# Seven y products behind the gates of a recurrent layer, and a front with its sines on GpSimd

## The chip, the cores and the metric

The kernel runs on one core of a Trainium2 chip, as one launch. The metric is the device time of that core in microseconds (us). The engines are named PE (TensorE), DVE (VectorE), ACT (ScalarE), POOL (GpSimd) and SP (SyncE, which here only starts transfers).

## What is computed

Two blocks act on 256 tokens of width 1024. The first has an attention layer with low-rank queries and keys (MLA), a state-space layer (SSM) and an MLP after each; each of the four parts has a shift, a scale and a gate that come from the vector c (modulation). The second has a recurrent layer, an attention layer and four feed-forward layers (f10, f20, f11, f21). Everything is fp32.

```python
def mla_mixer(h, cos, sin, w_in, q_norm, w_qb, kv_norm, w_kvb, w_o):
    z = h @ w_in                                  # 256 x (256 + 128 + 64)
    cq, ckv = rms_norm(z[..., :256], q_norm), rms_norm(z[..., 256:384], kv_norm)
    k_pe = apply_rope(z[..., 384:], cos, sin)
    # q from cq @ w_qb, keys and values from ckv @ w_kvb, 8 heads, causal softmax
    return o @ w_o

def rg_lru(x, w_r, b_r, w_i, b_i, lam):           # four heads of 256 x 256
    r, i = sigmoid(x @ w_r + b_r), sigmoid(x @ w_i + b_i)
    log_a = -LRU_C * r * softplus(-lam)
    u = sqrt(-expm1(2.0 * log_a)) * (i * x)
    return scan(exp(log_a), u)                    # along the tokens

def recurrent_block(xn, ...):
    xb, yb = split(xn @ w_in + b_in)
    h = rg_lru(causal_dwconv(xb, conv_w, conv_b), w_r, b_r, w_i, b_i, lam)
    return (h * gelu(yb)) @ w_out + b_out
```

## The kernel before, in words

All weights arrive as units of 128 x 1024 (512 KB), in one order that `plan()` writes down (L97). SP starts their transfers from one place, `_issue` (L404 to L418), into seven buffers `raw` taken in turn; a buffer is free again once its unit has been processed. `run` (L426) processes the next units: a unit "w" is split into a high half (`wh`, ACT, L458) and a low half (`wl`, DVE, L464; a few on POOL, L462), in a ring of eleven slots; a unit "m" of a modulation matrix is multiplied by silu(c) and summed on DVE (L522), which gives one column of shift, scale or gate; a unit "p" is a weight of the MLA front with a buffer of its own; a unit "x" stays in its raw buffer (`take_kept`). A product with split weights takes three matmuls: `wh` with the high half of the activations (`hh` or `xh`), `wl` with it, and `wh` with their low half (`hl` or `xl`). `step` and `take` (L474, L488) call `run` until a unit is there. What an engine does in which order follows from the program's order.

The front. `setup` (L946) makes silu(c), the decay of the SSM (`ssm_decay`, two powers on POOL), the angles and their sines and cosines (`sincos`, L909, on DVE, with Sin on ACT), the rope tables by 16 copies on POOL (L1001 to L1005), and the powers of the SSM's transition by 71 small operations on POOL (`ssm_powers`, L1281). `mla` (L1061) then takes eight pairs of modulation units; each pair gives one of eight groups of x, scaled, for PE's product with w_in. Norms of the result use `rpow` (L651), a power on POOL. Behind it stand on POOL the rotations of the SSM (`ssm_inputs`, L1351): tables of cosines and sines for two halves of the tokens, doubled in six steps of six operations each, 72 in all. SP stores them with `store` (L1355), at points that `tick` sets while the heads run. `ssm_tables` (L1333) turns the result of the powers by two transposes on PE (the wt transposes), and SP stores them.

The heads (`heads`, L1198) follow a string of tokens, `HEADS0`, repeated for each head with lags: T turn, S scores, B maximum (DVE), A product with the values, E exponential (ACT), N norm (L1231, DVE), q the next pair of queries with its rope, t a tick, and a number for so many calls of units. After them come the last product of the layer, mla_o (half 0 and half 1 of the tokens, eight weight units), a layer norm per half, and mlp0. Seven modulation units of `MODS0` (`MODS_PRE`) stand in the plan between mla_o and mlp0; the other 17 are woven into mlp0.

The recurrent layer (`lru`, L1744) follows `LRU_SEQ`. X evacuates the products of lru_x, C is the convolution (DVE, L1790), Y a pair of y products (PE, 32 matmuls with kept weights), R and I the gates (PE, then ACT), A weighs x by i (L1832), Q square roots (ACT), M scales (L1840, L1843), S is the scan (L1848), E evacuates y, G is its gelu (L1709 to L1711 on DVE, with ACT between), T multiplies the scan with gelu(y) and writes `hh` (L1853, L1854), L writes `hl` (L1859), J loads a row, and a number processes so many units, here of lru_out. The product with lru_out follows, half 0 and then half 1, each with an epilogue that begins at L708.

Of the kernel before, what the change touches and what calls it, by code (L numbers as in the profile page):

```python
# [36 lines left out]
LRU_SEQ = "X0 X1 C0 X2 C1 X3 Y0 E0 R0 I0 C2 R1 I1 C3 A0 R2 I2 A1 R3 I3 A2 Y1 Y2 Y3 H0 G0 A3 Q0 Q1 Q2 Q3 1 M0 S0 E1 M1 S1 G1 1 M2 S2 T0 T1 1 L0 E2 M3 S3 G2 1 L1 T2 J1 1 E3 G3 L2 1 J0 T3 J2 1 L3 1"  # L37
HEADS0 = "T2 S0 B0 1 A2 E0 N0 t q t 1"
# [46 lines left out]
LRU_W = _w("lru_x", 8) + [("x", "lru_y", 0), ("x", "lru_y", 1)] + [("x", "lru_" + c, k) for k in range(2) for c in "ri"]  # L85
LRU_W += [("x", "lru_y", k) for k in range(2, 8)] + _w("lru_out", 8)
MODS0 = _mod(2, 0) + _mod(2, 1) + _mod(1, 2)
MODS_AT = 8
MODS_PRE = 7
# [7 lines left out]
def plan():  # L97
# [218 lines left out]
class Model:  # L316
    def __init__(self, ctx, tc, ws, cols, rows, x, pos, inv, rel, sp, sbc, sgb, out):
# [30 lines left out]
        self.mhalf = T("mhalf", [128, 4])  # L348
        self.lri = T("lri", [128, 8], I32)
# [13 lines left out]
        self.pend = deque()  # L363
        self.kept = {}
# [3 lines left out]
        self.fill = 0  # L368

# [34 lines left out]
    def _issue(self, limit):  # L404
        while self.ndma < min(limit, len(UNITS)):
            j = self.ndma
            u = UNITS[j]
            if u[0] == "p":
                dst = self.pt[u]
            else:  # L410
                r = RPOS[j]
                if r >= RAWN and RUNITS[r - RAWN] >= self.nproc:
                    return
                dst = self.raw[r % RAWN]
                if any(dst is x for x, _ in self.pend) or any(dst is x for x in self.kept.values()):
                    return
# [9 lines left out]
    def run(self, look=LOOK, maxn=99, mods=2):  # L426
        n = 0
        while self.nproc < len(UNITS) and n < maxn:
# [4 lines left out]
            if u[0] == "m":  # L433
                if mods == 0 or (self.hold and self.modfin is not None):
                    break
                mods -= 1
# [4 lines left out]
            self.settle(KEEP)  # L441
            if u[0] == "w":
# [7 lines left out]
                if own is None and s >= RING - 3 and self.early:  # L450
                    break
# [11 lines left out]
                else:  # L463
                    self.nc.vector.tensor_tensor(self.Ls[s], raw, self.f32(self.Hs[s]), op=OP.subtract)  # L464
# [41 lines left out]

    def settle(self, keep):
# [401 lines left out]
    def sincos(self, s, c, ang, t1, t2):  # L909
        nc = self.nc  # L910
        tau = 2.0 * math.pi
# [3 lines left out]
        nc.vector.tensor_scalar(t1, ang, 1.0 / tau, MAGIC, op0=OP.mult, op1=OP.add)  # L915
        nc.vector.tensor_scalar(t1, t1, -MAGIC, None, op0=OP.add)
        nc.vector.scalar_tensor_tensor(t2, t1, -c1, ang, op0=OP.mult, op1=OP.add)
        nc.vector.scalar_tensor_tensor(t2, t1, -c2, t2, op0=OP.mult, op1=OP.add)
        nc.vector.scalar_tensor_tensor(t2, t1, -c3, t2, op0=OP.mult, op1=OP.add)
        nc.vector.tensor_scalar(t2, t2, 3.1415925, -3.1415925, op0=OP.min, op1=OP.max)  # L920
        nc.scalar.activation(s, t2, func=AF.Sin)
        nc.scalar.activation(t1, t2, func=AF.Sin, scale=0.5)
        nc.vector.scalar_tensor_tensor(t1, t1, -2.0, t1, op0=OP.mult, op1=OP.mult)
        nc.vector.tensor_scalar(c, t1, 1.0, None, op0=OP.add)
# [21 lines left out]
    def setup(self):  # L946
# [3 lines left out]
        spt = self.Z[1][:, 1664:1664 + NSP]  # L950
        inv = self.Z[1][:, 1600:1632]
# [12 lines left out]
        V.memset(self.mhalf, -0.5)  # L964
        jp = self.Z[0][:, 0:128]
# [14 lines left out]
        while self.nproc < 2:  # L980
            self.step()
        V.tensor_copy(self.identb, self.ident)
        V.tensor_copy(self.maskb, self.mask)
        posf = self.stat(2)
        V.tensor_copy(posf, posi)
        n = 64 + 7 * 32
        a, t1, t2 = (self.Z[1][:, n * i:n * i + n] for i in range(3))
        sc = self.Z[1][:, 3 * n:5 * n].rearrange("p (e a) -> p e a", e=2)
        for h in range(2):
            V.tensor_scalar(a[:, 32 * h:32 * h + 32], inv, posf[:, h:h + 1], None, op0=OP.mult)  # L990
        for e in range(7):
            V.tensor_scalar(a[:, 64 + 32 * e:96 + 32 * e], self.sw[2], float(1 << (e + 1)) if e else 1.0, None, op0=OP.mult)
        self.sincos(sc[:, 0], sc[:, 1], a, t1, t2)
        self.tok = self.sb.tile([128, 2, 2, 32], F32, name="tok")
        for e in range(2):
            G.tensor_copy(self.tok[:, e], sc[:, 1 - e, 0:64].rearrange("p (h f) -> p h f", h=2))
        CT, ST = self.B2, self.BR
        for h in range(2):
            for j in range(4):
                o = slice(128 * h + 32 * j, 128 * h + 32 * j + 32)  # L1000
                G.tensor_copy(CT[:, o], self.tok[:, 0, h])  # L1001
                if j % 2 == 0:
# [1046 lines left out]
```

## Time and profile before

| | us |
|---|---|
| median of three runs | 1716.37 |
| lowest and highest | 1714.93, 1719.49 |
| the profiled execution | 1720.69 |
| its span | 1718.9 |
| PE busy | 1602.1 (93%) |
| DVE busy | 1134.9 (66%) |
| ACT busy | 832.9 (48%) |
| POOL busy | 227.1 (13%) |

A busy share is a mean over stages. PE is busy nearly all the time, so a loss is a stretch in which PE is not, and a wait on another engine counts where PE waits behind it in the end. POOL's work lies almost wholly in the first 110 us. In the rows below, a bracket at the end of a row gives the idle time of that engine just before, and what ended it; xN joins equal instructions in a row.

### The profile page before, as it was taken

What the parts mean: (1) busy time and instruction counts of PE and PEld (TensorE: products, weight loads), DVE (VectorE), ACT (ScalarE), POOL (GpSimd) and SP (SyncE); (2) the same over time, 40 slices, a digit from 0 to 9 for tenths busy, and PEclk for the clock granted to TensorE, in tenths of its full rate; (3) what the DMA queues carried; (4) which work ended last, traced back from release to release, by engine and by line L of the source; (5) the groups of instructions that cost most, each with busy time, mean ns of one, the idle gap of its engine ahead of it and who ended that gap; (6) DMA issues with size and microseconds to landing.
All of it is one profiled execution on the core that took longest, in us unless ns stands there. A gap on an engine that the chain in (4) does not pass through costs nothing.

```text
span 1718.9 us, 24910 instructions
## 1 busy us (share of the span) xinstructions
PE 1602.1 (93%) x9594; PEld 1414.2 (82%) x9594; DVE 1134.9 (66%) x1596; ACT 832.9 (48%) x1256; POOL 227.1 (13%) x318
## 2 busy tenths in 40 slices
PE   4779999998789999999999889999999999899998
PEld 2557889887778899789997758999899998779997
DVE  6688898669978655776555577555755555775553
ACT  2333657745345655353444755444544444654341
POOL 8940000003514000100000011000000001320000
PEclk9869999998899999999999999999999999999999
DMA  9477688957566665475551446565555653545540
GB/s 363 173 271 261 222 290 297 316 191 281 208 220 231 234 216 192 146 248 206 191 175 51 161 170 241 193 208 181 187 180 194 222 199 109 184 143 205 205 147 26
DMA packets 106586, 349.62 MB, mean 203 GB/s; under 512 B 12385, under 2 KB 22753, under 8 KB 106466
## 3 DMA queue, kind: packets, MB, share of 16 engines
q1 hardware_dynamic: 106466, 348.02, 58.1%
q8 instruction: 75, 1.23, 0.3%
q14 instruction: 45, 0.37, 0.1%
HBM read 338.41 MB, written 9.57 MB: 202 GB/s over the span
## 4 chain that ended last, share of the span: by engine, by line
PE 49%; DVE 4%; ACT 3%; issue 2%; POOL 1%; DMA 0%; DVEq 0%; POOLq 0%; ACTq 0%
PE bank L395 48%; DVE wl L464 1%; ACT wh L458 1%; PE bank L611 1%; ACT junka L660 1%; DMA raw<-in_ws_dram 0%; DVE r L698 0%; ACT r L1815 0%; POOL wl L462 0%; ACT z L1816 0%; PE bank L877 0%; POOL st L656 0%; DVE z L1231 0%; DVE z L1848 0%; DVE st L1218 0%
## 5 line engine op out<-in xcount | busy, mean ns | idle before, releaser
L464 DVE TENSOR_TENSOR wl<-raw,wh 128x1024 fp32r<-128x1024 f32 x456 | 549.8, 1240 | 167.9 <-ACT wh L458 166.6
L458 ACT ACTIVATE wh<-raw 128x1024 fp32r<-128x1024 f32 x472 | 478.7, 1051 | 249.5 <-PE bank L395 129.9
L395 PE MATMUL bank<-xh,wh 128*128 128x256 f32 x1664 | 472.0, 284 | 0.0
L395 PE MATMUL bank<-xh,wl 128*128 128x256 f32 x1664 | 471.2, 283 | 0.0
L395 PE MATMUL bank<-xl,wh 128*128 128x256 f32 x1664 | 470.3, 283 | 0.0
L395 PEld LDWEIGHTS bank<-xl,wh 128*128 128x128 f32 x1664 | 318.9, 192 | 2.1
L395 PEld LDWEIGHTS bank<-xh,wh 128*128 128x128 f32 x1664 | 317.9, 191 | 2.4 <-issue 0.2
L395 PEld LDWEIGHTS bank<-xh,wl 128*128 128x128 f32 x1664 | 317.5, 191 | 0.0
L395 PE MATMUL bank<-wh,hh 128*128 128x512 f32 x736 | 295.5, 402 | 6.9 <-ACT hh L1854 3.6
L395 PE MATMUL bank<-wl,hh 128*128 128x512 f32 x736 | 292.9, 398 | 1.6 <-DVE wl L464 1.5
L395 PE MATMUL bank<-wh,hl 128*128 128x512 f32 x736 | 243.9, 397 | 7.2 <-DVE hl L1859 4.4
L395 PEld LDWEIGHTS bank<-wh,hl 128*128 128x128 f32 x736 | 140.0, 191 | 40.7 <-DVE hl L1859 6.3
L395 PEld LDWEIGHTS bank<-wh,hh 128*128 128x128 f32 x736 | 141.4, 192 | 38.2 <-ACT hh L603 4.3
L395 PEld LDWEIGHTS bank<-wl,hh 128*128 128x128 f32 x736 | 141.2, 192 | 31.3 <-DVE wl L464 2.9
L522 DVE SCALAR_TENSOR_TENSOR junk<-raw,cs 128x1024 bf16<-128x1024 f32 x96 | 124.4, 1296 | 10.8 <-DMA raw<-in_ws_dram 9.6
L395 PE MATMUL bank<-wl,xh 128*128 128x512 f32 x320 | 127.0, 397 | 2.2 <-DVE wl L464 1.3
L656 POOL TENSOR_TENSOR st<-st,mhalf 128x1 f32<-128x1 f32 (+1 forms) x33 | 22.8, 692 | 798.4 <-DVE st L664 696.5
L395 PE MATMUL bank<-wh,xh 128*128 128x512 f32 x320 | 127.6, 399 | 0.7 <-ACT wh L458 0.7
L604 DVE TENSOR_TENSOR hl<-z,hh 128x512 fp32r<-128x512 f32 x68 | 47.0, 692 | 100.5 <-ACT hh L603 100.5
L395 PE MATMUL bank<-wh,xl 128*128 128x512 f32 x320 | 102.3, 397 | 5.6 <-DVE xl L604 5.6
L603 ACT ACTIVATE hh<-z 128x512 fp32r<-128x512 f32 x68 | 43.0, 632 | 106.1 <-DVE z L896 105.1
L462 POOL TENSOR_TENSOR wl<-raw,wh 128x256 fp32r<-128x256 f32 x64 | 60.6, 979 | 128.5 <-ACT wh L458 128.3
(381 smaller groups left out, 1665.3 us busy)
## 6 DMA issues: line engine op xcount, KB each, us to landing
raw<-in_ws_dram SPq DMA_DIRECT2D x580, 512.0 KB
early<-in_ws_dram SPq DMA_DIRECT2D x10, 512.0 KB
grow<-in_rows_dram SPq DMA_DIRECT2D x9, 512.0 KB
brow<-in_rows_dram SPq DMA_DIRECT2D x6, 512.0 KB
ophh<-ops_d SPq DMA_DIRECT2D x6, 512.0 KB
ophl<-ops_d SPq DMA_DIRECT2D x6, 512.0 KB
gate<-in_rows_dram SPq DMA_DIRECT2D x5, 512.0 KB
tab_d<-early SPq DMA_DIRECT2D x4, 512.0 KB
```

Source lines behind the costliest of these rows:

```text
L395: self.nc.tensor.matmul(out, l, r, start=start, stop=stop)
L458: self.nc.scalar.activation(self.Hs[s], raw, func=AF.Copy)
L462: self.nc.gpsimd.tensor_tensor(self.Ls[s][:, w], raw[:, w], self.f32(self.Hs[s])[:, w], op=OP.subtract)
L464: self.nc.vector.tensor_tensor(self.Ls[s], raw, self.f32(self.Hs[s]), op=OP.subtract)
L522: nc.vector.scalar_tensor_tensor(self.junk, raw, 1.0, self.cs, op0=OP.mult, op1=OP.mult, accum_out=total)
L603: self.nc.scalar.activation(hdst, src, func=AF.Copy)
L604: self.nc.vector.tensor_tensor(ldst, src, self.f32(hdst), op=OP.subtract)
L611: self.nc.tensor.transpose(b[:, 128 * j:128 * j + 128], src[:, 128 * k:128 * k + 128], self.ident)
L656: self.nc.gpsimd.tensor_tensor(r, v, self.mhalf[:, 0:n], op=OP.pow)
L660: self.nc.scalar.activation(self.junka[:, 0:512], src, func=AF.Square, scale=scale, accum_out=s[:, n:n + 1])
```

## The change

It has five parts.

1. The recurrent layer. The eight units of lru_out become kept units ("x"), between those of y. One y product instead of two stands ahead of the gates, seven behind them; Y is now a single product. A new letter K splits a kept unit of lru_out: K0 to K3, among the gates, with both halves on DVE, K4 to K7 with the high half on ACT. E and G come later, and L (the low half of the product's left operand, the remainder) comes late.
2. The front. The angles are made on ACT, the sines and cosines on POOL (Sin stays on ACT), the rope tables by six copies on ACT. On POOL the first three steps of rotations of one half precede `rpow`; the other rotations, a power and the 71 operations follow it. SP stores the rotations after the heads. The wt transposes move from ahead of the heads to the norm of mla_o's half 0.
3. The plan. Modulation units, front weights and units of mla_o alternate; `MODS_PRE` is 0, so that all 24 units of `MODS0` are woven into mlp0.
4. The heads process three units per head, no ticks, and delay each low half of a weight to the next unit (`lag`); their norm goes to ACT.
5. The transposes ahead of kvk are issued together, six first, and the two for the roped key after kvk.

```diff
-LRU_SEQ = "X0 X1 C0 X2 C1 X3 Y0 E0 R0 I0 C2 R1 I1 C3 A0 R2 I2 A1 R3 I3 A2 Y1 Y2 Y3 H0 G0 A3 Q0 Q1 Q2 Q3 1 M0 S0 E1 M1 S1 G1 1 M2 S2 T0 T1 1 L0 E2 M3 S3 G2 1 L1 T2 J1 1 E3 G3 L2 1 J0 T3 J2 1 L3 1"
-HEADS0 = "T2 S0 B0 1 A2 E0 N0 t q t 1"
+LRU_SEQ = "X0 X1 C0 Y0 X2 C1 X3 R0 I0 C2 R1 I1 C3 A0 K0 K1 R2 I2 A1 R3 I3 K2 K3 A2 A3 Y1 Y2 Y3 Y4 Y5 Y6 Y7 H0 0 Q0 Q1 Q2 Q3 M0 S0 M1 S1 E0 G0 K4 M2 S2 T0 E1 G1 K5 M3 S3 T1 J1 K6 E2 G2 T2 J2 L0 L1 K7 L2 E3 G3 J0 T3 L3 1 1"
+HEADS0 = "T2 S0 B0 1 A2 E0 1 N0 q 1"
...
-MODS_PRE = 7
+MODS_PRE = 0
...
-    o += [("p", "kvk", 0), ("p", "kvv", 0)]
...
+    m, w = _mod(1, 0) + _mod(1, 1) + _mod(0, 2), _w("mla_o", 8)
+    o += m[:3] + [("p", "kvk", 0), ("p", "kvv", 0)] + m[3:8] + [("p", "qb", 0)] + m[8:10]
+    o += [("p", "qb", k) for k in (1, 2, 3)] + m[10:11]
+    m = m[11:]
+    for k in range(8):
+        o += [w[k]] + m[2 * k:2 * k + 2]
...
+    def split_kept(self, tag, k, eng):
...
+        if eng is None:
+            self.nc.scalar.activation(self.Hs[s], raw, func=AF.Copy)
+        else:
+            eng.tensor_copy(self.Hs[s], raw)
+        self.nc.vector.tensor_tensor(self.Ls[s], raw, self.f32(self.Hs[s]), op=OP.subtract)
...
-        nc.vector.tensor_scalar(t1, ang, 1.0 / tau, MAGIC, op0=OP.mult, op1=OP.add)
...
+        G.tensor_scalar(t1, ang, 1.0 / tau, MAGIC, op0=OP.mult, op1=OP.add)
+        G.tensor_scalar(t1, t1, -MAGIC, None, op0=OP.add)
+        for x in (c1, c2, c3):
+            G.tensor_scalar(t2, t1, -x, None, op0=OP.mult)
+            G.tensor_tensor(ang, ang, t2, op=OP.add)
...
-                G.tensor_copy(CT[:, o], self.tok[:, 0, h])
...
+            nc.scalar.activation(o, c.unsqueeze(1).to_broadcast([128, 4, 32]), func=AF.Copy)
...
         r = self.rpow(ss, 4)
-        next(gen)
+        self.rotations(0, range(3, 6))
+        self.rotations(1, range(6))
+        self.ssm_powers()
...
-        self.ssm_tables()
-        self.bg, self.bgt = gen, 0.0
-        self.tick(0.1, run=False)
...
         self.hold = True
+        self.lag = True
         self.heads(HEADS0, q_pair, qk, None, VV)
-        self.hold = False
+        self.lag = self.hold = False
+        self.rests()
+        self.put_tables()
...
         def norm(h):
+            if h == 0:
+                self.ssm_tables()
+                self.halves()
...
-                nc.vector.tensor_scalar(P[h % 3][:, w], P[h % 3][:, w], rc[:, i:i + 1], None, op0=OP.mult)
+                if bias is None:
+                    nc.scalar.activation(P[h % 3][:, w], P[h % 3][:, w], func=AF.Copy, scale=rc[:, i:i + 1])
```

POOL around rpow in the front (`st<-st,mhalf`; `early` and `rot` are rotation tables, `wide` holds temporaries). Before:

```order
L1327 MEMSET grow 128x32
L1329 COPY grow<-z_98 128x32
L1330 COPY grow<-z_98 128x32
L1329 COPY grow<-z_98 128x32
L1330 COPY grow<-z_98 128x32
L1329 COPY grow<-z_98 128x32
L1330 COPY grow<-z_98 128x32
L656 TENSOR_TENSOR st<-st,mhalf 128x4
L1362 MEMSET early_80 128x16
L1363 MEMSET early_81 128x16
L1354 TENSOR_TENSOR early_84<-early_80,spp 128x16
L1354 TENSOR_TENSOR early_84<-early_81,spp 128x16
```

Now:

```order
L1421 TENSOR_TENSOR rot_81<-wide_85 128x16x2
L1421 TENSOR_TENSOR wide_85<-rot_80,spp 128x64
L1421 TENSOR_TENSOR wide_85<-rot_81,spp 128x64
L1421 TENSOR_TENSOR rot_80<-wide_85 128x16x4
L1421 TENSOR_TENSOR wide_85<-rot_80,spp 128x64
L1421 TENSOR_TENSOR wide_85<-rot_81,spp 128x64
L1421 TENSOR_TENSOR rot_81<-wide_85 128x16x4
L689 TENSOR_TENSOR st<-st,mhalf 128x4
L1421 TENSOR_TENSOR wide_85<-rot_80,spp 128x128
L1421 TENSOR_TENSOR wide_85<-rot_81,spp 128x128
L1421 TENSOR_TENSOR rot_80<-wide_85 128x16x8
```

The powers (`z_98`, `grow`) stood ahead of rpow and no longer do; steps of the rotations with 64 columns now stand there.

PE in mla_o, where the products of half 0 (`bank_124`, `bank_125`) end and those of half 1 begin, now:

```order
L400 MATMUL bank_124<-wh_57_804,hh_86 128x512
L400 MATMUL bank_124<-wl_57_805,hh_86 128x512
L400 MATMUL bank_125<-wh_57_804,hl_87 128x512
L400 MATMUL bank_124<-wh_57_804,hl_87 128x512
L1404 MATMUL bank_126<-ident,grow 128x128 x2
L400 MATMUL bank_129<-wh_37_571,hh_86 128x512
L400 MATMUL bank_129<-wl_37_572,hh_86 128x512
L400 MATMUL bank_130<-wh_37_571,hh_86 128x512
L400 MATMUL bank_130<-wl_37_572,hh_86 128x512
```

The two transposes of `grow` are the wt transposes; before, they stood between kvv and the first queries:

```order
L395 MATMUL bank_125<-early_75,gate 128x512
L395 MATMUL bank_126<-early_75,gate 128x512
L1337 MATMUL bank_127<-ident,grow 128x128 x2
L395 MATMUL bank_128<-gate,early_76 128x256 x4
L395 MATMUL bank_129<-gate,early_76 128x256 x4
```

They have moved past the heads and past half 0 of mla_o.

DVE in the recurrent layer, from the last A but one (L1832, now L1887) on. Before:

```order
L1832 SCALAR_TENSOR_TENSOR grow<-grow,z_99 128x512
L1709 SCALAR_TENSOR_TENSOR brow<-brow,z_98 128x512
L1711 SCALAR_TENSOR_TENSOR z_98<-brow,z_98 128x512
L1832 SCALAR_TENSOR_TENSOR grow<-grow,z_99 128x512
L464 TENSOR_TENSOR wl_56_866<-raw_69,wh_56_865 128x1024
L1840 SCALAR_TENSOR_TENSOR z_100<-r_92,z_100 128x512
L1842 MEMSET r_92 128x1 x2
L1843 TENSOR_TENSOR b2row<-b2row,z_100 128x512
L1848 SCALAR_TENSOR_TENSOR z_100<-r_92,b2row 128x512
L1840 SCALAR_TENSOR_TENSOR z_100<-r_92,z_100 128x512
L1842 MEMSET r_92 128x1 x2
L1843 TENSOR_TENSOR b2row<-b2row,z_100 128x512
```

Now:

```order
L535 CAST wh_58_814<-raw_65 128x1024
L536 TENSOR_TENSOR wl_58_815<-raw_65,wh_58_814 128x1024
L535 CAST wh_59_904<-raw_67 128x1024
L536 TENSOR_TENSOR wl_59_905<-raw_67,wh_59_904 128x1024
L1887 SCALAR_TENSOR_TENSOR grow<-grow,z_97 128x512 x2
L1895 SCALAR_TENSOR_TENSOR z_98<-r_90,z_98 128x512
L1897 MEMSET r_90 128x1 x2
L1898 TENSOR_TENSOR b2row<-b2row,z_98 128x512
L1903 SCALAR_TENSOR_TENSOR z_98<-r_90,b2row 128x512
L1895 SCALAR_TENSOR_TENSOR z_98<-r_90,z_98 128x512
L1897 MEMSET r_90 128x1 x2
L1898 TENSOR_TENSOR b2row<-b2row,z_98 128x512
```

The gelu (L1709, L1711) and the first low half (L464) no longer stand ahead of the first M; two of the K splits (L535, L536) stand there instead, ahead of the last A.

## Rows read from the trace of the kernel before

**Rows 1.** Table of stretches: span, PE, PEld, DVE, ACT, POOL busy, PEclk, DMA share, GB/s.

```profile
0.00:46.00 46.00, 20.60 (x56) 11.49 (x56) 29.28 (x85) 9.58 (x17) 39.98 (x79) 1.00 0.94 366
...
67.00:132.00 65.00, 50.62 (x200) 36.91 (x199) 50.75 (x101) 22.53 (x59) 38.73 (x53) 0.75 0.57 211
...
200.00:300.00 100.00, 96.94 (x619) 87.48 (x617) 90.54 (x150) 63.03 (x100) 0.00 (x0) 0.98 0.80 270
...
937.00:1010.00 73.00, 62.94 (x264) 51.13 (x264) 47.21 (x76) 48.35 (x86) 0.00 (x0) 0.91 0.48 164
```

**Rows 2.** Timeline of PE in the front: start us, us, operation, idle before.

```profile
29.62 0.48 PE L1010 MATMUL bank<-ident,b2row 128*128 128x128 f32 x1 [5.02 <-POOL b2row L1001]
...
33.73 12.49 PE L395 MATMUL bank<-early,z 128*128 128x448 f32 x32
...
55.14 5.14 PE L395 MATMUL bank<-gate,early 128*128 128x256 f32 x16
...
69.42 0.70 PE L395 MATMUL bank<-brow,z 64*128 64x256 f32 x2 [1.60 <-DVE z L1170]
```

**Rows 3.** Timeline of DVE in the front.

```profile
12.03 0.39 DVE L990 TENSOR_SCALAR z<-z,st 128x32 f32<-128x32 f32 x2
...
17.23 1.22 DVE L522 SCALAR_TENSOR_TENSOR junk<-raw,cs 128x1024 bf16<-128x1024 f32 x1
...
31.38 1.23 DVE L522 SCALAR_TENSOR_TENSOR junk<-raw,cs 128x1024 bf16<-128x1024 f32 x1 [0.30 <-DMA raw<-in_ws_dram]
...
46.92 0.25 DVE L1094 TENSOR_SCALAR st<-st 128x2 f32<-128x2 f32 x1 [9.82 <-ACT junka L1092]
```

**Rows 4.** Timeline of POOL in the front.

```profile
9.03 5.44 POOL L1274 TENSOR_TENSOR z<-z 128x32 f32<-128x32 f32 x1
...
18.66 1.20 POOL L1001 COPY b2row<-tok 128x32 f32<-128x32 f32 x1
...
50.13 1.03 POOL L656 TENSOR_TENSOR st<-st,mhalf 128x4 f32<-128x4 f32 x1
```

**Rows 5.** Table of stretches for POOL's small operations and rotations.

```profile
29.70:36.90 7.20, 7.20 (x27) 5.70 (x28) 6.64 (x16) 4.00 (x8) 6.96 (x11) 1.00 1.03 410
37.00:50.00 13.00, 9.22 (x25) 4.37 (x23) 2.50 (x20) 2.25 (x9) 12.40 (x61) 1.00 1.01 403
51.10:108.30 57.20, 48.29 (x186) 34.60 (x187) 45.66 (x88) 17.98 (x48) 53.49 (x77) 0.82 0.42 151
```

**Rows 6.** Waits of SP's queue, 40 to 135 us: total, times, longest.

```profile
SPq L1355 <- POOL early L1354: 34.4, 4, 15.7
```

**Rows 7.** Groups of DVE, 67 to 132 us: busy, mean ns, idle before.

```profile
L522 DVE SCALAR_TENSOR_TENSOR junk<-raw,cs 128x1024 bf16<-128x1024 f32 x15 | 20.8, 1387 | 9.3 <-DMA raw<-in_ws_dram 9.3
L1231 DVE TENSOR_SCALAR z<-z,st 128x256 f32<-128x256 f32 (+1 forms) x16 | 9.7, 647 | 0.3
L464 DVE TENSOR_TENSOR wl<-raw,wh 128x1024 fp32r<-128x1024 f32 x6 | 7.3, 1224 | 1.4 <-ACT wh L458 1.2
```

**Rows 8.** Timeline of PE at mla_o and the border to mlp0.

```profile
132.40 0.77 PE L395 MATMUL bank<-wh,hh 128*128 128x512 f32 x1
...
160.64 1.22 PE L395 MATMUL bank<-wh,xl 128*128 128x512 f32 x2 [3.68 <-DVE xl L604]
```

**Rows 9.** Timeline of PE in the recurrent layer.

```profile
959.82 20.88 PE L395 MATMUL bank<-xt,raw 128*128 128x256 f32 x96
984.35 0.80 PE L395 MATMUL bank<-wh,hh 128*128 128x512 f32 x1 [3.65 <-ACT hh L1854]
```

**Rows 10.** Timeline of DVE in the recurrent layer.

```profile
970.35 1.23 DVE L464 TENSOR_TENSOR wl<-raw,wh 128x1024 fp32r<-128x1024 f32 x1 [3.15 <-ACT wh L458]
...
1005.20 0.68 DVE L1859 TENSOR_TENSOR hl<-z,hh 128x512 fp32r<-128x512 f32 x1
...
1010.34 1.28 DVE L708 TENSOR_TENSOR r<-bank,brow 128x512 f32<-128x512 f32 x2
```

**Rows 11.** Timeline of ACT in the recurrent layer: the last gates.

```profile
963.15 0.82 ACT L1823 ACTIVATE grow<-bank,cols 128x256 f32<-128x256 f32 x2
```

More of the change, by code (lines that the diff above doesn't have):

```diff
@@ L368, in __init__, with halves @@
         self.fill = 0
+    def halves(self):
+        self.XH, self.XL = (self.sb.tile([128, 8, 256], F32R, name=t, tag=t) for t in ("xh", "xl"))
     def hidden(self, i):
@@ L433, in run @@
             if u[0] == "m":
-                if mods == 0 or (self.hold and self.modfin is not None):
+                if mods == 0 or (self.hold and self.modfin is not None and u[1][4] == '2'):
                     break
@@ L449, in run @@
                     break
-                if own is None and s >= RING - 3 and self.early:
+                if own is None and not self.lent.get(s, set()) <= self.finished:
                     break
@@ L463, in run @@
                 else:
[L464 removed]
+                    self.plo.append((raw, s))
+                    if not self.lag:
+                        self.rests()
             elif u[0] == "m":
@@ L1114, in mla, with turn_z @@
         tb = [self.bank(), self.bank()]
-        for j in (2, 0, 1, 3):
+        def turn_z(js):
+            for j in js:
+                for half in range(2):
+                    nc.tensor.transpose(tb[half][:, 128 * j:128 * j + 128],
+                                        ZT[:, 512 * half + 128 * j:512 * half + 128 * j + 128], self.ident)
+        turn_z((2, 0, 1))
+        for j in (2, 0, 1):
             for half in range(2):
@@ L1137, in mla @@
         self.done(u)
-        self.run(maxn=5, mods=5)
+        turn_z((3,))
+        for half in range(2):
+            nc.scalar.activation(KP[:, 128 * half:128 * half + 128], tb[half][:, 384:512], func=Copy)
+        self.rel(*tb)
+        self.run(maxn=3, mods=3)
         u, w = self.take_raw("p", "kvv", 0)
@@ L1379, in store, with put_tables @@
+    def put_tables(self):
+        for b in range(2):
             for e in range(2):
                 d = self.tab_d[2 * b:2 * b + 2, :, 512 * e:512 * e + 512].rearrange("b p n -> p b n")
-                dma(d, tabs[b][e].rearrange("p (b n) -> p b n", b=2))
-        rotations(0, range(ROT))
-        yield 0.0
-        rotations(0, range(ROT, 6))
-        rotations(1, range(6))
-        yield ROT_T
-        store(0)
-        yield ROT_U
-        store(1)
-        self.early = None
+                self.nc.sync.dma_start(out=d, in_=self.tabs[b][e].rearrange("p (b n) -> p b n", b=2))
+        self.finished.add("tables")
```

213 lines of the change are left out of this document (116 added, 97 removed).

## The prediction

> **What bounds the kernel now.** I read the table of stretches first, to see where TensorE (PE) is not the limit. In [rows 1] PE is busy 20.60 of the first 46 us and 50.62 of the 65 us of the MLA heads, while from 200 to 300 us PE has 96.94 of 100 and VectorE (DVE) 90.54. So the front and the heads hold some 40 us in which PE does nothing, and mlp0 has little room on either engine. The recurrent layer is the other loose stretch: PE 62.94 of 73 us.
>
> Then the timelines, to see which wait ends last. On PE [rows 2] the transposes of the rope tables wait 5.02 us for copies on GpSimd (POOL) and start at 29.62; as they stand ahead of the rest on PE, the products with x start at 33.73, take 12.49 us, and kvk starts at 55.14. On DVE [rows 3] the sines begin at 12.03, the next pair of modulation sums at 17.23, and when the last sum is done DVE waits 9.82 us, until 46.92, for the norms of those products. On POOL [rows 4] a copy of 32 columns takes 1.20 us beside DVE's sums, a power 5.44, and rpow, which the norms need, starts at 50.13. So until 55 us the chain runs POOL, PE's late products, norms.
>
> In the heads the reader is to look at SP's queue: it waits 34.4 us in four pieces for POOL's rotations before it may store them [rows 6], and no weight behind the stores moves; DVE stands 9.3 us idle for raw units there [rows 7]. At the border to mlp0 PE waits 3.68 us for xl [rows 8]. In the recurrent layer PE waits 3.65 us for the first hh [rows 9]; on DVE [rows 10] the first low half of lru_out, at 970.35 after 3.15 us of waiting for ScalarE (ACT), stands ahead of the first M, and the last remainder L3 starts at 1005.20.
>
> **The change, part by part.** Times are of the profiled execution, 1720.69 us (span 1718.9), 4.3 above the median of 1716.37; the sum is made against it.
>
> *Front to kvk.* The rope copies leave POOL and the sines leave DVE. PE's products then follow the units as they come. DVE loses 5.2 us (12.03 to 17.23), but transfers bound the last pair: DVE already waits 0.30 us for a raw at 31.38 [rows 3]. So the last sum, which ended at 37.10 (46.92 less 9.82), gains 1 at most. Eight pairs make PE's 12.49 us; two of them, 3 us, are then left, and PE ends near 39 instead of 46.2. The norms keep their length, so rpow could start near 43. POOL must be free by then: it has a power of 5.44, eleven operations of the sines and 18 rotations ahead of it, from 9.5 on. At 1.2 us each that is 45, at half of it 27. I take -8 for rpow and, as the transposes for kvk are now grouped and the first ropes no longer stand behind ten sums (PE waited 1.60 us for them at 69.42 [rows 2]), **-10** for kvk and the first score. Bounds -5 and -12.
>
> *Heads.* Eight heads took 63 us (69.42 to 132.40 [rows 2, 8]). In the 65 us of [rows 1] DVE works 50.75, of which 9.7 are norms, with 21 units (15 sums, 6 low halves) [rows 7]. Now there are three units per head, 24, and no norm: 50.75 - 9.7 + 3 x 1.3 = 45. PE works 50.62 at a granted clock of 0.75, or 38 at full clock. ACT, busy 22.53, takes the norm; the trace has none on ACT, so I bound it by the whole sum on DVE, 9.7, and half of it: not the limit. SP has no store before the end of the heads, so the 9.3 us of waits go. With 45 on DVE and 38 to 51 on PE, and the handing on between engines, I take 56, -7; ends 0 (PE stays at the low clock) and -11. mla_o then starts near 115.
>
> *What POOL does meanwhile.* After rpow come 54 of the 72 rotations, then a power of 5.44 and 71 small operations that stood ahead of rpow. The 72 took 53.49 us [rows 5]; the 54 are the wider ones, so I take 46: 43 to 89, 94 with the power. The 71 must be bounded: 0.20 us each where DVE is nearly idle (12.40 us for 61), 0.63 beside dense sums (6.96 for 11) [rows 5]. So 14 to 45 us, an end from 108 to 139. I take 0.45, 32 us, an end near 127, since DVE has gaps in the heads. The two wt transposes, which need the result, now stand on PE behind half 0 of mla_o (11.1 us, counted from 132.40), so PE comes to them at 126: of the 17, **-15** is left, with -4 and -23 as ends.
>
> The Trainium skill, page "SBUF — State Buffer", section "SBUF: two separate sides", speaks against this part: it calls the port pair that GpSimd shares with VectorE an exclusive lock, held for a whole instruction by whichever starts first, and lists VectorE instructions with two inputs in SBUF among its takers. By that rule each POOL operation waits out a whole sum, which is rival A; the trace agrees in direction (0.63 against 0.20 us [rows 5]), but the mean is half of a sum.
>
> *Border.* The seven modulation units between mla_o and mlp0 go; they were 9 us of DVE just ahead of the xl for which PE waits 3.68 [rows 8]: **-3.5**, ends 0 and -3.7.
>
> *mlp0.* They come back inside: 7 x 1.3 = 9 us of DVE and 3.7 MB of transfers. DVE has 9.5 us free between 200 and 300 [rows 1], so most is hidden: **+3**, ends 0 and +9.
>
> *Recurrent layer.* One y product of 3.5 us (20.88 for six [rows 9]) moves from ahead of the gates to behind them. ACT ends the gates at 963.97 [rows 11]; it can start once X3 is done, some 2 us earlier, 962. K0 to K3 put four copies and four low halves on DVE there. The copy is not in the trace; by the low half of the same width, 1.23 [rows 10], I bound it by 1.23 and half of that, 7 to 10 us in all; DVE has 26 us free in this stretch [rows 1], much of it under the gates, and all hides. M0, which followed the low half at 970.35, so at 971.5, starts near 964. Behind it stand four low halves between the scans as before, but the remainders come at the end, and three low halves instead of four stand ahead of the epilogue that starts at 1010.34. Against it: E1 and G1 now follow the square roots on ACT and their table loads. L3 comes near 998 instead of 1005.20, the epilogue near 1002: **-8**, ends -4 and -11.
>
> Sum: -15 - 3.5 + 3 - 8 = -23.5; 1720.7 becomes 1697, the median **1693**. The good ends together give -38, the bad ones -4 + 0 + 9 - 4 = +1.
>
> **The rivals.** About 0.3%, 5 us, is what a measurement of this kernel can tell from no change.
>
> A. *POOL becomes the bound and the kernel is slower.* The 54 + 71 operations go at DVE's pace, and DVE is held by them in turn (sixteen norms took 9.7 us beside POOL and without, 0.65 each; sums 1.39 on average in the heads against 1.22 [rows 7, 3]). PE waits for wt ahead of half 1 of mla_o, SP stands behind it with the stores of wt, and mlp0's weights come late. Half 1 started at 143.5; with -3.5, +3 and -8 the break-even is POOL's end at 152. From 43, less the power, that is 103.6 us for 125 operations, **0.83 each**. [Rows 5] has 53.49/77 = 0.69 for the heads and 0.63 for the small ones. At 1.0 the end is 173, but DVE runs dry before and POOL speeds up; I put it at 160, +8, a median of 1724. For it: 1.20 for a copy of 32 columns [rows 4]. Against: 0.20 alone. Chance 0.08.
>
> B. *POOL late, but less*: an end near 140 leaves 1 to 4 us of the front's gain, so -11 in all, 1705. Chance 0.15.
>
> C. *The recurrent layer gives nothing*: E1 and G1 on ACT, or a low clock after PE's pause, hold L3 at 1005. -15.5, 1701. For it: the pause of 3.65 us stays if the first hh is no earlier. Chance 0.15.
>
> D. *The change moves the waits and no more*: POOL late as in B, +9 in mlp0, -4 in the recurrent layer; between -5 and +1, a median of 1714. Chance 0.10.
>
> E. *More*: the heads and the recurrent layer at their good ends and POOL early, 1682. Chance 0.12.
>
> **How the numbers follow.** The forecast's own case (1686 to 1698) has 0.40. With B, C and E it is 0.82 faster, of which 0.02 lies above 1711; D is no change but for 0.02 slower, A slower. So 0.80 faster, 0.10 the same, 0.10 slower. The range runs from 1676, a little below E, to 1713, which takes in B, C and part of D; A, the rest of D and the far good ends are left out.
>
> **What would show it.** No wait on PE ahead of the products, kvk near 45, rpow near 42; no wait of SP on POOL in the heads; mla_o from 113 to 117; PE's wait for the wt transposes under 3 us (over 15: A or B); no wait for xl at the border; L3 near 998, the epilogue of half 0 near 1002; mlp0 some 3 us longer. The forecast is wrong if the power operations on POOL average over 0.83 us, if mla_o starts after 125, or if L3 stays at 1005.

## The result: 1692 us, and the profile after

Five runs of the changed kernel have a median of 1692.20 us (1687.22 to 1694.99), five of the kernel before in the same series 1714.93; the ratio is 0.9857, 95% interval [0.9844, 0.9870]. The forecast was 1693. The profiled execution took 1692.64, with a span of 1690.9.

The powers of the norms (rpow on POOL, 33 of them) are the same in all kernels, so their starts divide the run into stages. Below, the change's lead over the kernel before at some of them, from the timelines of POOL and PE; the last column uses a second profile of the kernel before, taken with the experiments.

| | before | after | lead | lead, second profile |
|---|---|---|---|---|
| rpow of the front | 50.1 | 42.2 | 7.9 | 7.9 |
| first product of mla_o | 132.4 | 124.5 | 7.9 | 8.1 |
| norm of half 1 of mla_o | 166.0 | 153.8 | 12.2 | 12.0 |
| first norm behind mlp0 | 376.3 | 362.4 | 13.8 | 10.4 |
| last norm ahead of the recurrent layer | 919.9 | 903.8 | 16.2 | 12.6 |
| first norm behind it | 1013.5 | 991.9 | 21.6 | 18.0 |
| last norm of its half 1 | 1029.5 | 1008.0 | 21.6 | 19.6 |
| last norm of all | 1713.2 | 1685.9 | 27.3 | 25.2 |

So the front gave 7.9, the heads nothing, the border 4, mlp0 between -1.6 (it got longer) and +1.6, the recurrent layer 5.4 (1.6 more behind it against the second profile), and some 8 came from stages in which the sum had nothing. The two pairs of profiles differ by 27.3 and 25.2 us, the medians by 22.7.

One statement made of the kernel before is too strong: of the 227.1 us that POOL is busy, 98.4 lie in the first 110 us and 128.8 in later layers. The change leaves those as they were (128.1 us behind the first 126).

The timeline of PE, front to mla_o (the answer to [rows 2, 8]):

```profile
29.93 6.12 PE L400 MATMUL bank<-early,z 128*128 128x448 f32 x8 [3.26 <-ACT z L1126]
...
46.12 5.30 PE L400 MATMUL bank<-gate,early 128*128 128x256 f32 x16 [0.46 <-ACT gate L1184]
...
62.21 0.70 PE L400 MATMUL bank<-brow,z 64*128 64x256 f32 x2 [3.25 <-DVE z L1229]
...
93.25 1.65 PE L400 MATMUL bank<-z,z 128*128 128x256 f32 x4 [5.18 <-ACT z L1095]
...
124.47 0.48 PE L400 MATMUL bank<-wh,hh 128*128 128x512 f32 x1
...
135.62 0.38 PE L1404 MATMUL bank<-ident,grow 128*128 128x128 f32 x2
```

The products with x no longer stand behind the rope tables as a whole; kvk starts at 46.12 instead of 55.14, the first ropes at 62.21 instead of 69.42. A small rest is left: the last eight products, at 37.63, wait 1.14 us for z on ACT, which stands there behind the copy of the rope tables' transposes (L1060, at 36.52) although its sum was done at 35.15. From the first ropes to mla_o it is 62.3 us, against 63.0 before. The wt transposes at 135.62 wait for nothing.

The timeline of POOL, its rpow and the end of its powers (answers to [rows 4]):

```profile
42.25 1.04 POOL L689 TENSOR_TENSOR st<-st,mhalf 128x4 f32<-128x4 f32 x1 [2.10 <-DVE st L1149]
...
92.67 7.61 POOL L1354 TENSOR_TENSOR wide<-wide 128x32 f32<-128x32 f32 x2
...
125.39 0.21 POOL L1397 COPY grow<-wide 128x32 f32<-128x32 f32 x1
```

and the groups of DVE, first from 46 to 62 us, then in the heads, where the modulation sums, the low halves and the two groups with the longest idle time ahead of them are shown (answers to [rows 7]):

```profile
L555 DVE SCALAR_TENSOR_TENSOR junk<-raw,cs 128x1024 bf16<-128x1024 f32 x8 | 13.4, 1671 | 0.2
```

```profile
L555 DVE SCALAR_TENSOR_TENSOR junk<-raw,cs 128x1024 bf16<-128x1024 f32 x14 | 19.5, 1395 | 0.0
...
L504 DVE TENSOR_TENSOR wl<-raw,wh 128x1024 fp32r<-128x1024 f32 x9 | 12.9, 1430 | 1.8 <-ACT wh L464 1.8
...
L637 DVE TENSOR_TENSOR hl<-bank,hh 128x256 fp32r<-128x256 f32 x8 | 3.3, 418 | 4.4 <-ACT hh L636 4.4
...
L1227 DVE TENSOR_TENSOR z<-bank,brow 128x256 f32<-128x256 f32 x3 | 1.3, 425 | 5.7 <-PE bank L400 5.7
```

A sum that takes 1.22 us in [rows 3] takes 1.67 on average in the eight ahead of the first ropes, and 1.40 in the heads, as it did there before (1.39, [rows 7]). The long ones lie beside the rotations: beside POOL's small operations, from 101 us on, a sum takes 1.21 to 1.28. DVE's wait for raw units, 9.3 us in [rows 7], is gone, but it now waits 5.7 us for PE's products for the ropes and 4.4 for ACT's hh. In PE's table of waits over the whole run the longest entry is this one, all of it in the heads (L1095 copies the turned exponentials, ahead of their product with the values):

```profile
PE bank L400 <- ACT z L1095: 13.3, 5, 5.2
```

SP's waits for POOL (the answer to [rows 6]) are now those behind the heads:

```profile
SPq L1444 <- POOL wide L1354: 2.5, 3, 1.5
```

The recurrent layer on DVE (answers to [rows 10], with one of the new copies), and on PE:

```profile
936.15 0.69 DVE L535 CAST wh<-raw 128x1024 fp32r<-128x1024 f32 x1
...
948.81 0.69 DVE L1895 SCALAR_TENSOR_TENSOR z<-r,z 128x512 f32<-128x512 f32 x1 [1.25 <-ACT z L1891]
...
982.50 0.69 DVE L1914 TENSOR_TENSOR hl<-z,hh 128x512 fp32r<-128x512 f32 x1 [0.70 <-ACT hh L1909]
...
988.73 1.29 DVE L741 TENSOR_TENSOR r<-bank,brow 128x512 f32<-128x512 f32 x2 [1.79 <-PE bank L400]
```

```profile
941.39 24.34 PE L400 MATMUL bank<-xt,raw 128*128 128x256 f32 x112
...
976.27 1.22 PE L400 MATMUL bank<-wh,hl 128*128 128x512 f32 x2 [9.62 <-DVE hl L1914]
```

PE waits once, 9.62 us, where it had waited in pieces, of which [rows 9] shows the longest; the pieces came to 9.5 us in all. The first products behind it run at the lower of the two granted clocks (table of stretches):

```profile
976.30:981.20 4.90, 4.90 (x12) 3.84 (x13) 3.73 (x6) 2.91 (x5) 0.00 (x0) 0.50 0.81 332
981.80:988.40 6.60, 6.60 (x30) 5.36 (x30) 4.19 (x4) 3.48 (x4) 0.00 (x0) 1.00 0.77 262
```

### The profile page after: what moved, and what is told of

Its sections match the earlier page's. It is cut to its first block, busy times and chain, and to the rows that moved or that the text cites. A ratio compares the mean times of both kernels' runs of the same rounds, so it can differ in the third digit from the quotient of the medians.

```text
span 1690.9 us, 24901 instructions
## 1 busy us (share of the span) xinstructions
PE 1589.7 (94%) x9594; PEld 1400.8 (83%) x9594; DVE 1130.8 (67%) x1568; ACT 838.4 (50%) x1285; POOL 238.5 (14%) x309
## 4 chain that ended last, share of the span: by engine, by line
PE 49%; DVE 4%; ACT 3%; issue 1%; POOL 1%; DMA 0%; DVEq 0%; POOLq 0%; ACTq 0%
PE bank L400 48%; ACT junka L693 1%; DVE wl L504 1%; PE bank L644 1%; ACT wh L464 0%; DMA raw<-in_ws_dram 0%; DVE r L731 0%; ACT r L1870 0%; POOL wl L468 0%; DVE z L1844 0%; ACT z L1871 0%; POOL st L689 0%; DVE z L1300 0%; DVE z L1903 0%; DVE st L1284 0%
## 5 line engine op out<-in xcount | busy, mean ns | idle before, releaser
L504 DVE TENSOR_TENSOR wl<-raw,wh 128x1024 fp32r<-128x1024 f32 x448 | 538.8, 1236 | 161.9 <-ACT wh L464 159.9
L464 ACT ACTIVATE wh<-raw 128x1024 fp32r<-128x1024 f32 x464 | 471.6, 1051 | 246.1 <-PE bank L400 131.8
L400 PE MATMUL bank<-wh,hl 128*128 128x512 f32 x736 | 243.0, 396 | 13.3 <-DVE hl L1914 9.6
L555 DVE SCALAR_TENSOR_TENSOR junk<-raw,cs 128x1024 bf16<-128x1024 f32 x96 | 128.9, 1343 | 4.1 <-DMA raw<-in_ws_dram 2.9
```

The lines of the kernel that those rows point to most:

```text
L400: self.nc.tensor.matmul(out, l, r, start=start, stop=stop)
L464: self.nc.scalar.activation(self.Hs[s], raw, func=AF.Copy)
L555: nc.vector.scalar_tensor_tensor(self.junk, raw, 1.0, self.cs, op0=OP.mult, op1=OP.mult, accum_out=total)
```

## The experiments

Times are medians with the ratio to the kernel before on the same chip; the changed kernel's own ratio is 0.9857. Times of one kernel scatter over some 8 us, so the starts of the norms are compared too, stage by stage.

**POOL silent behind rpow (e5_pool_quiet).**

```diff
         for e in es:
             n, o = 1 << e, 32 * e + 16 * b
+            if e > 2 or b:
+                nc.gpsimd.memset(c[:, :, n:2 * n], 1.0)
+                nc.gpsimd.memset(s[:, :, n:2 * n], 0.0)
+                continue
```

(and memsets in place of the powers.)

> The changed kernel without the rotations from the fourth step of the first half on and without the powers: POOL writes constants there instead, so the SSM layer gets other numbers. POOL is then idle from about 46 us on. Theory: POOL slows DVE's two-input work (sums and low halves in the heads 1.40 and 1.43 us on average against 1.22), which is 4 to 5 us in the heads and 3 to 4 us in the sums ahead of the first ropes: first product of mla_o 6 to 8 us earlier, 1685. Rival: the heads are bound by the handing on between PE, ACT and DVE, and mla_o starts at most 2 us earlier, 1691.

1682.76, ratio 0.9811 [0.9790, 0.9832]. First ropes at 58.8 instead of 62.2, mla_o at 115.3 instead of 124.5, so 3.4 of it ahead of the heads and 5.8 in them. The groups of DVE in its heads:

```profile
L555 DVE SCALAR_TENSOR_TENSOR junk<-raw,cs 128x1024 bf16<-128x1024 f32 x14 | 17.1, 1218 | 0.0
...
L504 DVE TENSOR_TENSOR wl<-raw,wh 128x1024 fp32r<-128x1024 f32 x9 | 11.0, 1222 | 2.3 <-ACT wh L464 2.3
```

Both are at 1.22 us. The table of stretches of its heads (span, PE, PEld, DVE, ACT, POOL busy, PEclk, DMA share, GB/s):

```profile
58.80:115.30 56.50, 45.22 (x198) 33.82 (x199) 38.90 (x84) 31.17 (x78) 0.00 (x0) 0.83 0.75 264
```

The theory holds, with somewhat more than it said, but not all of it need be DVE's work. The granted clock is 0.83 here against 0.75 in the changed kernel, and PE is busy 3.8 us less; whether the clock rose because the waits fell, or for another reason, is not shown. The same heads beside a working POOL took between 60.0 and 65.1 us in six profiles (see the heads' order below), so in the heads POOL costs 3.5 us at the least, with one profile of this kernel.

**Silu(c) in PSUM (e11_cs_psum).** POOL's work is untouched; only the second operand of the sums moves.

```diff
-        self.banks = [ps.tile([128, 512], F32, name="bank%d" % i) for i in range(8)]
+        self.banks = [ps.tile([128, 512], F32, name="bank%d" % i) for i in range(6)]
+        self.pair = ps.tile([128, 1024], F32, name="pair")
+        self.banks += [self.pair[:, 0:512], self.pair[:, 512:1024]]
...
-            nc.vector.scalar_tensor_tensor(self.junk, raw, 1.0, self.cs, op0=OP.mult, op1=OP.mult, accum_out=total)
+            nc.vector.scalar_tensor_tensor(self.junk, raw, 1.0, self.cs if self.csp is None else self.csp, op0=OP.mult, op1=OP.mult, accum_out=total)
...
```

(and two copies of silu(c) into `pair` on ACT, ahead of kvk.)

> The changed kernel with silu(c) copied to two PSUM banks ahead of kvk, so that the modulation sums from there to the end of the heads read one operand from SBUF and one from PSUM. Theory (DVE and POOL get into each other's way where DVE reads two operands from SBUF): the sums between 46 and 61 us go from 1.37 to 2.16 us each back to 1.22, those in the heads from 1.40 to 1.22, POOL gets faster too, though the low halves still read two operands from SBUF; first ropes 3 us and mla_o 4 to 6 us earlier, 1687. Rival 1: what POOL slows is not the second read from SBUF; the sums stay at 1.4 and more, 1692. Rival 2: a read of PSUM is slower than one of SBUF, sums at 1.4 to 2 us everywhere, also where POOL is done, 1695.

1712.09, ratio 0.9974 [0.9963, 0.9985]: far slower than the changed kernel, and yet clear on the question. DVE's groups from 42 to 140 us:

```profile
L558 DVE SCALAR_TENSOR_TENSOR junk<-raw,pair 128x1024 bf16<-128x1024 f32 x22 | 26.7, 1213 | 1.6 <-ACT pair L1193 1.4
...
L507 DVE TENSOR_TENSOR wl<-raw,wh 128x1024 fp32r<-128x1024 f32 x15 | 19.5, 1316 | 7.1 <-ACT wh L467 6.1 <-DMA tab_d<-rot 1.0
```

The sums are at 1.21 us although POOL works beside them; the low halves, with two operands in SBUF, still take 1.32 (1.38 in the heads alone). POOL's powers end at 103.6 instead of 125.6. So DVE and POOL get into each other's way through DVE's second operand in SBUF. mla_o starts at 117.1, 7.4 earlier. The first sum starts at 49.29 instead of 46.38, behind the two copies, so the first ropes come no earlier. The heads take 54.9 us at a high granted clock:

```profile
62.20:117.10 54.90, 43.84 (x199) 32.79 (x199) 40.29 (x84) 30.96 (x78) 39.24 (x93) 0.88 0.79 270
```

In e12, whose front and heads are the same, they take 57.4 at a clock of 0.80. By the norms the kernel then loses its lead and 18 us more, 12.4 of them in the last stage (f21, 186.3 us against 173.9) and 2 to 4 each in mlp0, the SSM, the recurrent layer and the stage of 222 us behind it. Waits that the changed kernel does not have stand in the table of PE's waits over the whole run:

```profile
PE pair L403 <- DVE z L1774: 12.7, 2, 11.4
...
PE pair L403 <- DVE z L932: 6.5, 5, 3.0
...
PE pair L403 <- DVE r L750: 3.6, 1, 3.6
```

The same table of the changed kernel has none of the three, nor any wait for two banks: here the two are one tile for the whole program, and products into `pair` wait for its readers. The second entry lies in f21, and makes 6.5 of the 12.4 us there; the 12.7 lie in the SSM, which gets only 4 longer. What the rest of the loss is made of is not shown. Separate tiles behind the heads might keep the gain; no run shows it.

**The heads' order (e3_norm_dve, e6_two_units, e8_norm_first).** The norm on DVE for all heads; the token string cut to two units; the norm ahead of the second unit:

```diff
-HEADS0 = "T2 S0 B0 1 A2 E0 1 N0 q 1"
+HEADS0 = "T2 S0 B0 1 A2 E0 N0 q 1"
...
-HEADS0 = "T2 S0 B0 1 A2 E0 1 N0 q 1"
+HEADS0 = "T2 S0 B0 1 A2 E0 N0 1 q 1"
```

> The changed kernel with the norm of the MLA heads on DVE again. Theory: the heads turn around DVE (in the rounds without queries it is busy 9.6 of 10 us), so the norm's 0.55 us for a pair alone and up to 2.16 beside POOL come back eight times: the first product of mla_o 4 to 10 us later, 1696 to 1702. Rival: the norm on ACT stands behind a split of 1.05 us there and lengthens the way from the exponential to the turn; then DVE's norm costs nothing or gains 1 to 4 us, 1688 to 1692.

> The changed kernel with two units per head instead of three. Theory: DVE sets the rounds of the heads, so eight units fewer take 8 to 10 us out of the heads; PE then waits for weights of mla_o, whose splits come behind, and gets most of it back: 1690 to 1696 in all, mla_o starting near 116. Rival: the heads are bound by the handing on, mla_o starts at 122 to 124 as now, and the units left over make it 4 to 8 us slower, 1697 to 1700.

> The changed kernel with the norm ahead of the second unit of a round, so that on ACT it follows the exponential and does not stand behind a split of a weight. Theory (DVE sets the rounds): no change beyond 1 us. Rival (the handing on from ACT to PE sets them): up to 1 us in each of eight heads, mla_o 3 to 8 us earlier, 1685 to 1689.

1692.70 (0.9871 [0.9837, 0.9905]), 1695.67 (0.9889 [0.9866, 0.9911]) and 1696.46 (0.9887 [0.9862, 0.9913]). From the first ropes to mla_o they take 60.0, 65.5 and 65.9 us. But six profiles whose heads are the changed kernel's take 62.3, 64.5, 60.1, 60.0, 65.1 and 64.5 (after, e1, e2, e4, e7, e10), so one program of heads ends anywhere from 60 to 65 us (e7 has another front; the other five are the same up to mla_o). Two of them as tables of stretches, after and e2_rest_early:

```profile
62.20:124.50 62.30, 49.02 (x199) 36.58 (x199) 44.93 (x84) 31.28 (x78) 59.32 (x103) 0.75 0.67 222
```

```profile
61.90:122.00 60.10, 46.36 (x199) 34.84 (x199) 43.97 (x84) 31.35 (x78) 57.21 (x99) 0.81 0.68 234
```

The granted clock is 0.75 in the one and 0.81 in the other. The heads of e3_norm_dve and of e6_two_units:

```profile
62.40:122.40 60.00, 45.62 (x197) 34.13 (x198) 50.23 (x100) 25.37 (x62) 57.11 (x98) 0.83 0.67 228
```

```profile
61.10:126.60 65.50, 48.80 (x198) 36.30 (x199) 40.26 (x82) 29.85 (x76) 56.38 (x111) 0.75 0.52 175
```

DVE works 50.2 us in the one and 40.3 in the other, and the one with more work is the shorter. So DVE's busy time does not set the heads' time, against the theory of e3, which expected at least 4 us, and that of e6. The norm's place on DVE or ACT cannot be told from the scatter. With two units the last product with the values starts 2.9 us earlier (116.86 against 119.79), 1.1 of it from the start of the heads, but PE then waits 4.67 us for the gate, whose sums come late: the theory's 8 to 10 us are not there. What DVE is spared turns into idle time, with 10.2 us of waits for the ropes' products where the changed kernel has 5.7. The norm first is no gain either.

**The sines on DVE (e7_sines_dve).** `sincos` as before, on DVE, the rest of the changed front kept.

> The changed kernel with the sines on DVE again (the rope tables stay on ACT, the order of POOL's work stays). Theory: in the changed kernel DVE waits 2.9 us in all for transfers between its sixteen sums, so of the 3.7 us that the sines take there only 1 to 2 reach the last sum, and kvk moves by as much: +1 to +2, 1694. Rival 1: the sines stand fully on the path: +4 to +5, 1697. Rival 2: POOL, 14 us of work lighter ahead of its rotations, lets DVE run freely in the front, and the time falls by 2 to 4, 1689.

1693.49, ratio 0.9876 [0.9847, 0.9905]. rpow comes 0.4 us later (42.7), the first ropes 0.4 later. DVE has no wait for a raw left in the front, so the sines fill waits, as the theory said. The 0.4 us are within the scatter: the same front has its rpow between 41.1 and 43.4 in the runs e1 to e4, e6, e8 and e10. So the sines' place is worth no more than about a microsecond. What is left for the front's gain is that the copies and the powers no longer stand ahead of PE and of rpow; the timelines show those waits gone, but no run put these two back.

**Seven modulation units at the border (e4_mods_border).**

```diff
-MODS_PRE = 0
+MODS_PRE = 7
```

> The changed kernel with seven modulation units at the border between mla_o and mlp0 again. Theory: the border gained 3.9 us by their absence and mlp0 pays next to nothing for them, so +3 to +4, 1696, with PE waiting for xl at the border again. Rival: mlp0 pays for them with DVE's time, so that it is 2 to 6 us shorter when they are gone from it, and the sum is 0 or negative, 1688 to 1692.

1690.21, ratio 0.9858 [0.9834, 0.9882]. The timeline of its PE has the wait again:

```profile
150.32 1.22 PE L400 MATMUL bank<-wh,xl 128*128 128x512 f32 x2 [3.47 <-DVE xl L637]
```

From the norm of half 0 to that of half 1 of mla_o it takes 17.4 us against 13.5, so the border had gained 3.9, as the theory said; but from there to the first norm behind mlp0 it takes 202.3 against 208.7 (206.0 to 211.0 in seven other kernels with 24 units in mlp0). The units cost about 6 there (4 to 9 by the scatter): the rival is right, and moving them is no gain. With these seven at the border, mlp0 took 210.3 and 207.2 in the two profiles of the kernel before, and 202.3 here and in e10; what made it 5 to 8 us shorter apart from the units is not shown.

**The recurrent layer as before (e1_lru_old).** Its order, units and pairs of y products from the kernel before.

> The changed kernel with the recurrent layer of the kernel before (its order, its units, pairs of y products). Theory: the layer is worth what the time between the norms on either side of it lost, 5.4 us, and nothing behind it, so +5.4 on the changed kernel's 1692.2, 1698, with every norm behind the layer 5 to 6 us later and none ahead of it moved. Rival 1: all by which the two profiles draw apart from the layer to the end, 11 us, is its work: 1703. Rival 2: it is worth nothing, the order of the layer being hidden: 1692.

1701.31, ratio 0.9914 [0.9885, 0.9944]. Its heads ended on the long side (3.2 us behind the changed kernel ahead of the layer). The layer itself is 6.7 us longer, and the stage behind it 1.6: 8.3, between the theory and rival 1, nearer to the forecast than the 5.4 of the first pair of profiles. The 1.6 are not the order's alone: with the old order that stage takes 16.0 us in the first profile of before and 17.6 in the second and in e1, against 16.0 in the changed kernel. The layer itself scatters too, from 86.1 to 89.0 us in the seven kernels with its new order (after and e3 to e8); the old order took 93.5 us twice and 94.8 in e1. So its gain is some 4.5 to 8.7 us.

**Remainders early (e2_rest_early).**

```diff
-... K4 M2 S2 T0 E1 G1 K5 M3 S3 T1 J1 K6 E2 G2 T2 J2 L0 L1 K7 L2 E3 G3 J0 T3 L3 1 1"
+... K4 M2 S2 T0 E1 G1 L0 K5 M3 S3 T1 J1 K6 E2 G2 L1 T2 J2 K7 L2 E3 G3 J0 T3 L3 1 1"
```

> The changed kernel with the remainders L0, L1, L2 of the recurrent layer moved forward, each behind the gelu that follows its T. Theory: in the changed kernel PE waits 9.62 us for L0 and then works without a pause for 12.2 us to the end of half 0, so the late L0 sets the end and not the last scan; early remainders let PE do two or three units before, and the end comes 2 us earlier, 1690. Rival: DVE's chain of scans sets it, and three operations of 0.69 us pushed ahead of it make it 1 to 2 us later, 1694.

1689.50, ratio 0.9856 [0.9829, 0.9883]. From the last norm ahead of the layer to the first behind it, 86.6 us against 88.1: 1.5 less, as expected. But e3, e5, e6 and e8, with the late remainders, took 87.1, 87.4, 87.4 and 86.1 us there, so these 1.5 are within the scatter. The wait of 9.62 us falls apart into one of 2.87 for the first hh and one of 2.98 for L0, and yet e8, which has the long wait, is no slower. So late remainders are no visible part of the layer's gain, and no cost of theirs is shown; neither the theory nor the rival can be told.

**Two and three edits together (e10_both, e12_all).**

> The changed kernel with the seven modulation units at the border again and the early remainders, without PSUM. Theory: -2 and -1.6 add up, 1688.5. Rival: both were within the scatter of the heads' end, and the time is the changed kernel's, 1692.

> The changed kernel with three edits together: silu(c) in PSUM as in the run before, the seven modulation units at the border again, and the remainders of the recurrent layer early. Theory: they lie in different stages and add up: -5 (PSUM), -2 (border and mlp0 together), -1.6 (recurrent layer), 1684. Rival: the heads end as before their clock lets them, and only -3 to -4 is left, 1688.

1693.29, ratio 0.9865 [0.9850, 0.9879], and 1716.18, ratio 1.0000 [0.9982, 1.0018]. In e10 the layer takes 86.6 again and mlp0 202.3, but its heads took 64.5; the rival holds. e12 carries the two joined banks of e11 and their waits: the theory's 1684 is missed by 32 us. No version that does all the work is faster than the changed kernel beyond the scatter.

**The kernel before once more (c_before).**

> The kernel before, profiled once more. The profile on record has 683.6 us from the last norm of the recurrent layer to the last norm of all, the changed kernel 677.9. Theory: the change does nothing to that part, and a second profile of the kernel before shows 678 to 680 there. Rival: the change shortens it, and the second profile has 683 again.

1718.44 in one run, and 683.6 us again from the last norm of the recurrent layer to the last of all. All kernels made from the changed one but those with joined banks have 677.9 to 679.4 there, e1 with the old layer among them. The rival is right: this part is shorter, although the change moves nothing in it. Groups of PE in f21, of c_before and then of after:

```profile
L395 PE MATMUL bank<-xh,wl 128*128 128x256 f32 x288 | 81.5, 283 | 0.0
...
L395 PE MATMUL bank<-wh,hh 128*128 128x512 f32 x78 | 30.7, 393 | 0.2 <-ACT hh L603 0.2
```

```profile
L400 PE MATMUL bank<-xh,wl 128*128 128x256 f32 x288 | 80.9, 281 | 0.0
...
L400 PE MATMUL bank<-wh,hh 128*128 128x512 f32 x78 | 30.8, 394 | 0.2 <-ACT hh L636 0.2
```

The 864 products of 128 x 256 in this stage take 281 ns instead of 283, and their starts follow each other 117.9 ns apart instead of 120.0, with the granted clock at 1.00 and 0.25 us of waits in both: 173.9 us for 176.6. That spacing makes 1.8 of the 2.7 us; e1, e2, e8 and e10, with the same 281 ns, have 175.0. The other four stages that are filled with such products, between mlp0 and the recurrent layer and behind it, are 0.5, 1.4, 1.3 and 1.3 us shorter, with spacings of 118.2 to 118.7 instead of 119.9 to 120.0. What makes them so stays open. None of the parts undone in the experiments brings 283 back; the late allocation of the tiles xh and xl, which stand in these products and now share a place with tables of the front, and the plan by turns were not undone.

## Why the prediction was right, and where only its total was

*Front.* -8 for rpow: measured -7.9. -10 for kvk: -9.0. The sum that had POOL free at 27 to 45 does not hold the 5.44 us of the power that it names (with it, 32 to 50); POOL was free at 40.2, 2.1 us before rpow needed it, so this did no harm. For the first ropes -10 became -7.2: the eight sums ahead of them took 1.67 us, and with POOL silent the ropes come 3.4 us earlier (e5), of which 1.0 lies ahead of kvk already. The step had not priced POOL's rotations beside these sums.

*Heads.* This is the step that failed: -7 forecast, 0.7 measured (63.0 to 62.3 us). Its parts came out. DVE's work was forecast at 45 us and is 44.93, with sums at the 1.39 us of [rows 7], so what POOL costs a sum was in it; SP's waits for POOL are down from 34.4 [rows 6] to 2.5, and DVE's 9.3 us of waits for raw units are gone. What failed is the overlap: that the heads would shrink to 56 us once these waits went, with DVE idle for 11. It is idle for 17.3, now for PE and ACT, and PE is busy 49.0 us and waits 13.3 for ACT's copy of the turned exponentials. e3 and e6 show that the time does not follow DVE's work. The step had named its bad end itself, 0 if PE stays at the low clock, and the granted clock was 0.75, as before (0.74). Without POOL beside them, or with one operand of the sums in PSUM, the heads take 56.5 and 54.9 us, at clocks of 0.83 and 0.88. That 56 was forecast is luck: DVE works 38.9 and 40.3 us there, not 45. How much of these gains is DVE's shorter work and how much the clock stays open. The Trainium skill ("SBUF — State Buffer", section "SBUF: two separate sides") had the rule that speaks against the change, that a VectorE instruction with two inputs in SBUF and a GpSimd instruction that reads SBUF hold each other up; I used it for rival A, where POOL becomes the bound. The runs agree with it on DVE's side: 1.67 and 1.40 us with the second operand in SBUF, 1.21 with it in PSUM.

*POOL.* An end near 127 was forecast; it is 125.6. The 54 rotations took 49.4 us (46 forecast), the power 6.3 (5.44), the small operations 0.39 us each (0.45). The average over both is 0.61, under the 0.83 of rival A, and PE never waits for wt, since PE itself is late: it comes to them at 135.62 and not at 126.

*Border and mlp0.* -3.5 against -3.9, and +3 against 6 by e4: mlp0's term was inside its range but at half its size. Against the two profiles of before, mlp0 as a whole got 1.6 shorter or 1.6 longer even so; what made up for the units is not shown.

*Recurrent layer.* With the lead of 16.2 us taken off, the gates end at 963.0 (962 forecast), M0 starts at 965.0 (964), L3 at 998.7 (998), the epilogue at 1004.9 (1002). K's copies take 0.69 us and hide. -8 was forecast; 5.4 in the first pair of profiles, 6.7 to 8.3 in e1. The epilogue is late because PE, once L0 is there at 976.27, works 12.2 us without a pause to the end of half 0, the first 4.9 at a granted clock of 0.50 and the rest at 1.00. That is the low clock behind PE's pause that rival C named. That earlier remainders would bring the end forward is not shown: e2 gains no more than the scatter.

*The rest.* The sum had 0. Between mlp0 and the layer 2.4 us came, and behind the layer 5.7 (2.2 and 5.6 against the second profile); 7.2 of the 8.1 lie in the five stages of faster products, whose cause is open. They make up for the heads. The total of -23.5 against -22.7 is so in part luck: the mechanism was right in the front, at the border, in the recurrent layer and, at half its size, in mlp0, and a gain that is not there and one that was not foreseen are of nearly one size. Against the profiles that the sum was made for, the change is larger than forecast, 28.05 us (1720.69 to 1692.64).

## What to carry to other kernels

Before work is moved to GpSimd to relieve VectorE, count the VectorE instructions that read two operands from SBUF in that stretch: here a sum lost 0.18 to 0.45 us on average to GpSimd, and silencing GpSimd brought mla_o 9.2 us forward (6.7 against the profile with the earliest mla_o), more than the whole change of the heads' order. Taking a wait or some work from an engine shortens a stretch only if that engine sets it: here DVE lost its waits for weights and got others, for PE and ACT. Work that stands on an engine ahead of what others wait for, as the powers stood ahead of rpow, can go behind it; where it lands is a price of its own. A total that agrees with a forecast proves little about its terms: marks that all kernels share, such as the 33 norms here, show which terms hold.

## What the runs showed of the hardware beyond that

A sum with its second operand in PSUM took 1.21 us beside a busy GpSimd, against 1.40 to 1.67 with both in SBUF. The same heads behind the same front took 62.3 to 64.5 us at a granted clock of 0.74 to 0.75 in three profiles and 60 at 0.81 in two; which of the two makes the other is not shown. And products of 128 x 256 took 281 ns in one family of kernels and 283 in another at the same clock; the five stages that they fill got 7.2 us shorter, a quarter of the 27.3 between the two profiles.
